# Moving the f operand loads and the result stores of a down projection from SyncE's DMA queue to GpSimd's

## Chip, cores and metric

The kernel runs on one core of one Trainium2 chip. The metric is the device time of one execution in microseconds (us), and the smaller one is better. Engines are called as in the profile: PE is TensorE (PEld its weight loads), DVE is VectorE, ACT is ScalarE, POOL is GpSimd, SP is SyncE. SP computes nothing here: its program is a list of DMA issues in a fixed order. POOL can issue DMAs as well.

## The reference

One decoder layer, float32, for 512 tokens of width 2048: two attention mixers with a residual, then a feed-forward part with a gated causal convolution. The change lies in the last product of the second part.

```
D_MODEL = 2048; SEQ = 512; D_FF = 5632

def conv_ffn(h, w_up, w_conv, b_conv, w_down):
    S = h.shape[1]
    u = h @ w_up
    up = jnp.pad(u, ((0, 0), (CONV_W - 1, 0), (0, 0)))
    conv = b_conv
    for j in range(CONV_W):
        conv = conv + w_conv[j] * up[:, j:j + S]
    gate, val = jnp.split(conv, 2, axis=-1)
    return (jax.nn.silu(gate) * val) @ w_down
...
    x = x + gt_a * y                                   # after the mixers
    h = rms_norm(x, g_ffn[l]) * (1.0 + sc_f) + sh_f
    x = x + gt_f * conv_ffn(h, w_up[l], w_conv[l], b_conv[l], w_down[l])
```

Below, f is `silu(gate) * val`, 5632 x 512, stored with features on the partitions.

## The kernel before

**Number format.** Every float32 operand is split into a rounded part hi and a rest lo (`split`: ACT writes hi on L130, DVE writes lo = operand - hi on L131), and each product is three matmuls (L1082 to L1084: hi x hi, hi x lo, lo x hi). So each weight and each activation passes ACT and DVE before TensorE can use it. The splits of weights appear as `whi` and `wlo` in the profile, those of f operands as `slot<-slot`.

**The product scheme.** `seven` computes a 2 x 2 block product with seven block products instead of eight, in the manner of Strassen. One `Pair` covers two blocks of 128 output rows by 512 tokens. It loads four raw weight blocks (`load`, L968, on SP's queue), forms sums of them on DVE (`comb`, L981), splits the seven results, and runs seven steps on TensorE. After each step the result leaves the PSUM bank: ACT copies (L985 here, L987 in the up projection) or DVE adds (L991, L993). `seven` prepares the weights of a step `AHEAD` steps before that step, here 3. The right-hand operands are seven combinations of f (`KINDS`: r11, t3, t2, r21, t1, t4, r22), each 128 x 256 per block of the contraction.

**Up projection.** As each pair of f tiles is complete, `f_out` (stores on L1397 and L1406) writes f and its combinations to DRAM tiles `f_d` from POOL's queue.

**Down projection.** The contraction of 5632 is cut into four chunks (`DH` = 5, 6, 6 and 5 double blocks). For each chunk the eight column pairs are run in turn, `down_pair(c, j)`: 8 x 7 = 56 steps a chunk, in the order of `KINDS` within a pair. At the end of a pair, `fin` adds its two tiles into DRAM (`x1_d`) by an accumulating DMA from POOL (L1553). In the last chunk, x1 is loaded back (L1544, POOL), added (L1550, DVE), and the result is stored to `out` (L1551).

**The f operands.** A chunk's split operands stay in SBUF during its 56 steps, in tiles from a common pool of slots (`get` and `put`; a tile put back may be taken again after some steps). `ahead` is called after every step. It calls `load_tile` (L1482: up to two DMAs of 128 x 256 from `f_d` into one slot) and `split_tile` (L130 and L131 into two further slots) for the tiles of this and the next chunk. A load is asked for up to nine tiles ahead; a split is made no earlier than four steps after its load, unless the operand is due in two steps or less. In the last steps of a chunk the operands of that chunk become free one kind after the other (`held_by`), and the loads and splits for the next chunk pile up around that place.

**Order.** The program is written as above, but every engine's own order is decided by a planner (`TileContext(nc, schedule_with_timeline_sim=True)`) from its estimates of durations. Each engine and each DMA queue then runs its list strictly in order, and a DMA whose slot is not yet free holds up everything behind it in its queue. Weights (`raw<-in_w_down`), f loads and result stores share SP's list; stores of f, accumulates and x1 loads share POOL's.

The switch from up to down is `turn()`: it lays out seven raw buffers and four pairs of hi and lo buffers, of 768 columns each, for the weights.

Of the kernel before, what the change touches and what calls it, by code (L numbers as in the profile page):

```python
# [18 lines left out]
P = 128  # L19
T = 512  # L20
D = 2048
KD = D // P
# [9 lines left out]
def trunk_layer_kernel(  # L32
# [21 lines left out]
    V, A, G, PE, SP = nc.vector, nc.scalar, nc.gpsimd, nc.tensor, nc.sync  # L54
# [14 lines left out]
    def get(dt=F32):  # L69

        i = min(free, key=lambda n: rested[n])
        free.remove(i)
        if cur[i] is None or cur[i].dtype != dt:
            cur[i] = pool.tile([P, T], dt, name=f"slot{i}", tag=f"slot{i}")
        held[id(cur[i])] = i
        return cur[i]

    def getr():
        return get(F32R)

    def put(*ts, lag=2):

        for t in ts:
            i = held.pop(id(t))
            rested[i] = clock[0] + lag
            free.append(i)
# [126 lines left out]
    def late_loads():  # L213
        SP.dma_start(posi, rows(positions))
        for j in range(3):
# [17 lines left out]
                    base=0, pattern=[[-1, P]], channel_multiplier=1)  # L233
# [35 lines left out]
    for ks in (range(0, 7), range(7, 14), range(14, KD)):  # L269
# [4 lines left out]
        for k in ks:  # L274
            t = get()
# [112 lines left out]
    for g in range(-2, 8):  # L388
# [7 lines left out]
        if 0 <= g + 1 < 8:  # L396
            ada_cols(g + 1)
            for k in (2 * g + 2, 2 * g + 3):
                hi, lo, t = getr(), getr(), ht[k % 2]
# [138 lines left out]
    for tb in range(1, 4):  # L538
        S = (tb + 1) * P
        qiT = []  # L540
        for cb in range(2):
            t = qi[tb, cb]
# [4 lines left out]
            o = (getr(), getr())  # L547
# [60 lines left out]
    for tb in range(4):  # L608
        t = kva[tb]
# [299 lines left out]
    HT = T // 2  # L909
# [188 lines left out]
    for i in range(KH // 2):  # L1098
        raw = [get() for _ in range(4)]
        ta, tb_ = get(), get()  # L1100
        for j in range(2):
            k, o = 2 * i + j, slice(j * HT, (j + 1) * HT)
# [262 lines left out]
    for k in range(KD):  # L1365
        t = x1T[k]
# [23 lines left out]
    f_d = [[dram.tile([P, T if n else HT], F32, name=f"f{n}_{i}") for n in range(4)] for i in range(NF_ // 2)]  # L1390
# [79 lines left out]
    base = [sum(DH[:c]) for c in range(len(DH))]  # L1470
# [5 lines left out]
    def load_tile():  # L1476
        c, n, i = tiles.popleft()
        t = get()
        m, o = KEPT[n]
        w = min(2, DH[c] - i)  # L1480
        for e in range(w):
            SP.dma_start(t[:, e * HT:(e + 1) * HT], f_d[base[c] + i + e][m][:, o * HT:(o + 1) * HT])  # L1482
        coming.append((c, n, t, w * HT, clock[0]))

    def split_tile():
# [10 lines left out]
    def ahead(step, last):  # L1496

        first = [sum(56 for _ in DH[:c]) for c in range(len(DH))]

        def due(c, n):  # L1500
            return first[c] + KINDS.index(n) - step

        for late in (False, True):
            if coming and coming[0][0] <= last:
                c, n, _, _, at = coming[0]
                if due(c, n) <= 2 or not late and clock[0] >= at + 4 and rests(4) and len(free) >= 2 + KEEP \
                        and (due(c, n) < 12 or step % 2 == 0):
                    split_tile()
        for _ in range(2):
            if tiles and tiles[0][0] <= last:  # L1510
                c, n, _ = tiles[0]
                if due(c, n) <= 5 or len(coming) < (9 if due(c, n) < 24 else 4) and rests(3) and len(free) > KEEP:
                    load_tile()
# [22 lines left out]
    def down_pair(c, j):  # L1536
        ns = (2 * j, 2 * j + 1)
        x1 = []

        def load(blk):  # L1540
            if c == len(DH) - 1 and not x1:
                for n in ns:
                    x1.append(get())
                    G.dma_start(x1[-1], x1_d[n])  # L1544
            return w_downs[c][j, blk]

        def fin(*us):
            for i, (n, u) in enumerate(zip(ns, us)):
                if x1:
                    V.tensor_tensor(u, u, x1[i], ALU.add)  # L1550
                    SP.dma_start(out[n * P:(n + 1) * P, :], u)  # L1551
                else:
                    G.dma_start(x1_d[n], u, accum_op=ALU.add)  # L1553
            put(*us, lag=6)
            put(*x1)

        o = ops[c]
        return Pair(tuple(o[n] for n in ("r11", "r21", "r22", "t1", "t2", "t3", "t4")), load, fin, K=DH[c],
                    scale=tuple(mod[:, 80 + n:81 + n] for n in ns))
# [75 lines left out]
```

## Time and profile before

| | |
|---|---|
| median of 3 runs | 2737.32 us (2736.68 to 2745.78) |
| the profiled execution's own time | 2737.34 us |
| its span in the profile | 2735.6 us |
| mean granted TensorE clock | 0.985 |
| busy: PE, DVE, ACT, POOL | 2629.2, 2182.8, 1281.8, 272.0 us |
| f loads (`slot<-f`, L1482, SP) | 154 of 128 KB |
| weights of the down projection (L968, SP) | 64 of 384 KB and 64 of 320 KB |
| accumulates (L1553, POOL) | 48 of 256 KB |
| result stores (L1551, SP) | 16 of 256 KB |
| last f load of the profile issued at | 2608.4 us |

TensorE is busy for 96% of the span, but that is an average: the question for this change is what it does in the stretches in which it pauses. The down projection begins at about 2222 us, when the last step of the up projection has freed the weight buffers. A timeline row gives start, duration, engine, line, operation, tiles and shapes; in brackets stands how long the engine had been idle before the instruction, and what ended that wait. For the queues SPq and POOLq the duration is that of issuing, with consecutive issues of one kind put together.

### The profile page before, as it was taken

Reading aid. Unit: us, or ns where it says so; the run is one execution under the profiler, and the core shown is the slowest. Engines: PE = TensorE matmul, PEld = TensorE weight load, DVE = VectorE, ACT = ScalarE, POOL = GpSimd, SP = SyncE. Lnnn points to the kernel's source line nnn. Section 1 sums busy time; section 2 is a strip of 40 time slices with the busy share of each in tenths; the row PEclk is TensorE's granted clock in tenths of the full one; section 3 lists DMA queues with packets and bytes.
Section 4 is the critical chain, followed back from the end, with each engine's and each line's share of the span. In section 5 each row is a group of like instructions: output and inputs, shape, how many; then the busy total and the mean of one; then the engine's idle time right before and its main releaser. Section 6 shows DMA issues by size and latency. Waiting matters only on the chain.

```text
span 2735.6 us, 45476 instructions
## 1 busy us (share of the span) xinstructions
PE 2629.2 (96%) x17200; PEld 2359.1 (86%) x17200; DVE 2182.8 (80%) x3669; ACT 1281.8 (47%) x2069; POOL 272.0 (10%) x495
## 2 busy tenths in 40 slices
PE   6999999999999999999999999999999988898999
PEld 5787687779997767788789999999999978898999
DVE  7977967698878667973878888889898986777777
ACT  4333434334454465322545555555555564545444
POOL 1001011110032222100100000000000001010110
PEclk8999999999999999999999999999999999999999
DMA  9943136665585578952333333333334365756563
GB/s 339 339 152 105 29 113 214 208 198 177 196 251 163 169 257 289 336 192 96 137 117 132 120 125 129 124 125 135 123 129 142 119 205 142 194 135 182 137 199 114
DMA packets 236240, 464.33 MB, mean 170 GB/s; under 512 B 24330, under 2 KB 85412, under 8 KB 236020
## 3 DMA queue, kind: packets, MB, share of 16 engines
q1 hardware_dynamic: 199348, 368.79, 41.6%
q0 software_dynamic: 36640, 92.63, 12.1%
q8 instruction: 134, 2.20, 0.3%
q14 instruction: 86, 0.70, 0.1%
q10 hardware_dynamic: 32, 0.01, 0.0%
HBM read 397.11 MB, written 64.23 MB: 169 GB/s over the span
## 4 chain that ended last, share of the span: by engine, by line
PE 55%; issue 21%; DVE 11%; DMA 9%; POOL 2%; ACT 1%; SPq 0%; POOLq 0%; DVEq 0%; ACTq 0%
PE bank L134 10%; PE bank L135 10%; PE bank L136 10%; PE bank L1082 7%; PE bank L1083 7%; PE bank L1084 7%; DMA raw<-in_w_ups 4%; DVE wlo L131 4%; DMA slot<-in_w_ada 2%; POOL x L1553 1%; DVE raw L981 1%; DVE slot L981 1%; DVE slot L1380 1%; DMA raw<-in_w_down 1%; PE bank L1233 1%
## 5 line engine op out<-in xcount | busy, mean ns | idle before, releaser
L1082 PE MATMUL bank<-slot,whi 128*128 128x256 f32 x3920 | 1114.6, 285 | 61.7 <-ACT whi L130 17.9
L1083 PE MATMUL bank<-slot,whi 128*128 128x256 f32 x3920 | 1107.2, 283 | 0.2 <-DVE slot L131 0.2
L1084 PE MATMUL bank<-slot,wlo 128*128 128x256 f32 x3920 | 1097.4, 283 | 2.9 <-DVE wlo L131 2.8
L1082 PEld LDWEIGHTS bank<-slot,whi 128*128 128x128 f32 x3920 | 748.7, 191 | 77.7 <-ACT whi L130 19.9
L1083 PEld LDWEIGHTS bank<-slot,whi 128*128 128x128 f32 x3920 | 748.4, 191 | 0.7 <-DVE slot L131 0.5
L1084 PEld LDWEIGHTS bank<-slot,wlo 128*128 128x128 f32 x3920 | 742.6, 191 | 4.2 <-DVE wlo L131 4.1
L130 ACT ACTIVATE whi<-raw 128x1024 fp32r<-128x1024 f32 (+2 forms) x458 | 424.4, 928 | 463.9 <-PE bank L1083 367.9
L131 DVE TENSOR_TENSOR wlo<-raw,whi 128x1024 fp32r<-128x1024 f32 (+2 forms) x458 | 481.3, 1056 | 60.8 <-ACT whi L130 59.2
L122 ACT ACTIVATE whi<-raw 128x1024 fp32r<-128x1024 f32 (+4 forms) x182 | 187.4, 1031 | 389.2 <-PE bank L136 202.3
L123 DVE TENSOR_TENSOR wlo<-raw,whi 128x1024 fp32r<-128x1024 f32 (+4 forms) x182 | 215.6, 1186 | 145.4 <-ACT whi L122 140.1
L981 DVE TENSOR_TENSOR raw<-raw,raw 128x1024 f32<-128x1024 f32 (+2 forms) x252 | 264.7, 1051 | 71.1 <-DMA raw<-in_w_down 44.2
L135 PE MATMUL bank<-wlo,slot 128*128 128x512 f32 (+2 forms) x768 | 297.4, 388 | 0.9 <-DVE wlo L123 0.9
L134 PE MATMUL bank<-whi,slot 128*128 128x512 f32 (+2 forms) x768 | 289.9, 390 | 6.6 <-ACT slot L401 4.0
L136 PE MATMUL bank<-whi,slot 128*128 128x512 f32 (+2 forms) x768 | 292.3, 384 | 0.0
L135 PE MATMUL bank<-slot,whi 128*128 128x512 f32 (+1 forms) x656 | 262.9, 401 | 1.4 <-DVE slot L703 1.3
L134 PE MATMUL bank<-slot,whi 128*128 128x512 f32 (+1 forms) x656 | 260.9, 403 | 3.3 <-ACT slot L1370 2.3
L136 PE MATMUL bank<-slot,wlo 128*128 128x512 f32 (+1 forms) x656 | 257.5, 401 | 0.0
L134 PEld LDWEIGHTS bank<-whi,slot 128*128 128x128 f32 x768 | 146.0, 190 | 37.8 <-ACT slot L401 4.1
L135 PEld LDWEIGHTS bank<-wlo,slot 128*128 128x128 f32 x768 | 146.3, 191 | 29.5 <-DVE wlo L123 1.4
L136 PEld LDWEIGHTS bank<-whi,slot 128*128 128x128 f32 x768 | 145.1, 189 | 28.5 <-issue 0.3
L739 DVE SCALAR_TENSOR_TENSOR slot<-slot,c_act,slot 128x512 f32<-128x512 f32 x203 | 148.9, 746 | 24.9 <-DMA slot<-in_w_ada 23.9
L130 ACT ACTIVATE whi<-slot 128x512 fp32r<-128x512 f32 x204 | 128.1, 629 | 82.9 <-PE bank L1083 63.3
(292 smaller groups left out, 3007.1 us busy)
## 6 DMA issues: line engine op xcount, KB each, us to landing
slot<-in_w_ada SPq DMA_DIRECT2D x344, 256.0 KB, 5.7
raw<-in_w_ups SPq DMA_DIRECT2D x126, 512.0 KB, 4.4
raw<-in_w_in SPq DMA_DIRECT2D x50, 512.0 KB, 3.6
raw<-in_w_down SPq DMA_DIRECT2D x64, 384.0 KB, 4.0
raw<-in_w_down SPq DMA_DIRECT2D x64, 320.0 KB, 3.7
slot<-f SPq DMA_DIRECT2D x154, 128.0 KB, 3.4
slot<-in_w_ups SPq DMA_DIRECT2D x68, 256.0 KB, 2.6
f<-slot POOLq DMA_DIRECT2D x66, 256.0 KB, 5.3
```

Of the source, the lines that this page charges most:

```text
L122: A.activation(hi, raw[:, :w], AF.Copy)
L123: V.tensor_tensor(lo, raw[:, :w], r32(hi), ALU.subtract)
L130: A.activation(dst_hi, src, AF.Copy)
L131: V.tensor_tensor(dst_lo, src, r32(dst_hi), ALU.subtract)
L134: PE.matmul(o, lh, rh, start=first, stop=False)
L135: PE.matmul(o, lh, rl, start=False, stop=False)
L136: PE.matmul(o, ll, rh, start=False, stop=last)
L739: V.scalar_tensor_tensor(acc, ts[i], c_act[:, k:k + 1], acc, op0=ALU.mult, op1=ALU.add)
L981: V.tensor_tensor(part(o, x, y), part(a, x, y), part(b, x, y), op)
L1082: PE.matmul(o, wh[:, ks], rh, start=first and k == 0, stop=False, skip_group_check=True)
L1083: PE.matmul(o, wh[:, ks], rl, start=False, stop=False, skip_group_check=True)
L1084: PE.matmul(o, wl[:, ks], rh, start=False, stop=last, skip_group_check=True)
```

## The change

The loads of f operands (L1482) are issued by POOL (`G`) in place of SP. The result stores of the last chunk (L1551) are issued by POOL too, but for those of the last column pair, which stay on SP. Nothing else of the program text changes. SP's list falls by 168 instructions (154 f loads and 14 stores), and POOL's grows by 168. As the planner sees other queues, it also orders ACT, DVE and PE somewhat differently from the end of the up projection on; the instructions themselves are the same in number and shape.

```
@@ -1479,7 +1479,7 @@
         m, o = KEPT[n]
         w = min(2, DH[c] - i)
         for e in range(w):
-            SP.dma_start(t[:, e * HT:(e + 1) * HT], f_d[base[c] + i + e][m][:, o * HT:(o + 1) * HT])
+            G.dma_start(t[:, e * HT:(e + 1) * HT], f_d[base[c] + i + e][m][:, o * HT:(o + 1) * HT])
         coming.append((c, n, t, w * HT, clock[0]))
 
     def split_tile():
@@ -1548,7 +1548,7 @@
             for i, (n, u) in enumerate(zip(ns, us)):
                 if x1:
                     V.tensor_tensor(u, u, x1[i], ALU.add)
-                    SP.dma_start(out[n * P:(n + 1) * P, :], u)
+                    (SP if j == KD // 2 - 1 else G).dma_start(out[n * P:(n + 1) * P, :], u)
                 else:
                     G.dma_start(x1_d[n], u, accum_op=ALU.add)
             put(*us, lag=6)
```

More of the change, by code (lines that the diff above doesn't have):

```diff
@@ L1481, in load_tile @@
         for e in range(w):
-            SP.dma_start(t[:, e * HT:(e + 1) * HT], f_d[base[c] + i + e][m][:, o * HT:(o + 1) * HT])
+            G.dma_start(t[:, e * HT:(e + 1) * HT], f_d[base[c] + i + e][m][:, o * HT:(o + 1) * HT])
         coming.append((c, n, t, w * HT, clock[0]))
@@ L1550, in fin @@
                     V.tensor_tensor(u, u, x1[i], ALU.add)
-                    SP.dma_start(out[n * P:(n + 1) * P, :], u)
+                    (SP if j == KD // 2 - 1 else G).dma_start(out[n * P:(n + 1) * P, :], u)
                 else:
```

## The prediction

> **What bounds the kernel now.** I read the busy time by stretch first, for the stage that holds the moved transfers: the end of the up projection and the down projection, from 2200 us to the end. The columns are the stretch, its length, then busy time of PE, PEld, DVE, ACT and POOL, the granted TensorE clock, the DMA share and GB/s.
>
> ```profile
> 2200.00:2240.00 40.00, 30.50 (x227) 28.76 (x226) 38.32 (x60) 29.46 (x53) 1.63 (x3) 0.91 0.73 228
> 2240.00:2300.00 60.00, 50.23 (x385) 49.15 (x386) 41.57 (x62) 24.52 (x41) 6.58 (x8) 0.94 0.57 136
> 2350.00:2400.00 50.00, 43.45 (x319) 42.57 (x320) 39.40 (x54) 25.02 (x41) 5.15 (x6) 0.90 0.69 176
> 2400.00:2470.00 70.00, 68.23 (x567) 67.45 (x566) 51.59 (x66) 34.23 (x53) 6.82 (x8) 1.00 0.62 153
> 2470.00:2510.00 40.00, 32.39 (x234) 31.77 (x233) 28.59 (x43) 21.52 (x38) 3.41 (x4) 0.87 0.72 202
> 2600.00:2650.00 50.00, 45.01 (x359) 44.19 (x360) 35.40 (x52) 23.75 (x40) 12.29 (x20) 0.97 0.72 213
> 2650.00:2735.60 85.60, 81.19 (x681) 80.80 (x680) 67.76 (x101) 39.59 (x67) 0.00 (x0) 0.99 0.37 123
> ```
>
> Inside a chunk TensorE is the bound: 68.23 us busy of 70, at clock 1.00. What can be won lies where it isn't. I put the loss of a stretch at its idle time plus (1 - clock) times its busy time. That is 9.5 + 2.7 = 12.2 us for 2200 to 2240 (up turns into down), 9.8 + 3.0 = 12.8 for 2240 to 2300 (start of chunk 0), 6.6 + 4.3 = 10.9 for 2350 to 2400 (chunk 0 to 1), 7.6 + 4.2 = 11.8 for 2470 to 2510 (chunk 1 to 2), and 5.0 + 1.4 = 6.4 for 2600 to 2650 (chunk 2 to 3). In the last stretch 4.4 us are idle, almost all behind the last matmul.
>
> Next, the timeline of PE: its pauses in those stretches, each with what ended it in brackets.
>
> ```profile
> 2249.62 0.39 PE L1082 MATMUL bank<-slot,whi 128*128 128x256 f32 x1 [2.18 <-ACT whi L130]
> 2261.92 0.39 PE L1082 MATMUL bank<-slot,whi 128*128 128x256 f32 x1 [2.72 <-DVE slot L991]
> ...
> 2352.16 0.58 PE L1082 MATMUL bank<-slot,whi 128*128 128x256 f32 x1 [3.35 <-DVE slot L991]
> 2364.89 0.41 PE L1082 MATMUL bank<-slot,whi 128*128 128x256 f32 x1 [1.90 <-ACT slot L985]
> 2372.59 0.39 PE L1082 MATMUL bank<-slot,whi 128*128 128x256 f32 x1 [1.89 <-ACT whi L130]
> 2488.34 0.58 PE L1082 MATMUL bank<-slot,whi 128*128 128x256 f32 x1 [3.32 <-ACT whi L130]
> 2502.27 0.58 PE L1082 MATMUL bank<-slot,whi 128*128 128x256 f32 x1 [3.53 <-ACT slot L985]
> 2638.32 0.58 PE L1082 MATMUL bank<-slot,whi 128*128 128x256 f32 x1 [2.58 <-DVE slot L991]
> ```
>
> DVE and ACT end the pauses, so I ask what these two had waited for. First the table of waits from 2200 us on (us in total, times, longest), then the rows of the longest ones.
>
> ```profile
> POOL x L1553 <- DVE slot L991: 271.9, 24, 17.2
> DVE raw L981 <- DMA raw<-in_w_down: 44.2, 28, 4.4
> ACT slot L130 <- DMA slot<-f: 30.2, 15, 5.8
> ```
> ```profile
> 2350.02 0.96 DVE L981 TENSOR_TENSOR raw<-raw,raw 128x768 f32<-128x768 f32 x1 [3.53 <-DMA raw<-in_w_down]
> 2371.17 0.63 ACT L130 ACTIVATE slot<-slot 128x512 fp32r<-128x512 f32 x1 [5.82 <-DMA slot<-f]
> 2486.93 0.63 ACT L130 ACTIVATE slot<-slot 128x512 fp32r<-128x512 f32 x1 [4.49 <-DMA slot<-f]
> ```
>
> Before 2352 a weight came late for L981; before 2364 to 2373 and before 2488 ACT stood at the split of an f tile for a chunk that PE had not reached, with splits of weights that PE needed at once behind it in ACT's order. The timeline of the DMA queue on SP, and one row of POOL, says why those transfers were late.
>
> ```profile
> 2255.39 0.80 SPq L1482 DMA_DIRECT2D slot<-f  x2
> 2256.30 15.73 SPq L968 DMA_DIRECT2D raw<-in_w_down  x4
> ...
> 2337.22 7.04 SPq L1482 DMA_DIRECT2D slot<-f  x8
> 2344.36 0.86 SPq L968 DMA_DIRECT2D raw<-in_w_down  x2
> ...
> 2368.50 1.74 SPq L1482 DMA_DIRECT2D slot<-f  x4
> 2370.34 15.51 SPq L968 DMA_DIRECT2D raw<-in_w_down  x6
> ```
> ```profile
> 2362.99 0.86 POOL L1553 DMA_DIRECT2D x<-slot  x1 [3.20 <-ACT slot L985]
> ```
>
> The waits of the same queue name the cause of the gap before 2368.50:
>
> ```profile
> SPq L1482 <- DMA x<-slot: 30.8, 10, 5.8
> ```
>
> Two forms of one thing: f loads in front of weights. Eight f loads took 7.04 us to issue, and the weights whose lateness DVE shows at 2350.02 came out only then. From 2362.99 to 2368.50 the next f load waited (5.8 us at most, ten times in all) for the accumulate issued at 2362.99 to finish reading the slot that it writes, and six weights queued behind it. The same pattern stands at 2255.39, with four weights behind.
>
> **The change, part by part.** The 154 f loads (L1482) leave SP for POOL. The issue rows, in ns (min/median/max), and the time from issue to landing in us:
>
> ```profile
> L1482 SPq DMA_DIRECT2D slot<-f x154: 319/382/1457, 2045.7 to 2608.4; - x154
> L1406 POOL DMA_DIRECT2D f<-slot x66: 542/542/556, 1409.4 to 2241.7; - x66
> ```
> ```profile
> slot<-f SPq DMA_DIRECT2D x154, 128.0 KB, 3.4
> ...
> slot<-x POOLq DMA_DIRECT2D x16, 256.0 KB, 6.6
> ```
>
> SP loses 154 x 0.382 = 59 us of issuing, POOL gains 154 x 0.542 = 83 us, with room: POOL issued for 6.8 us in the 70 us from 2400. Landing on POOL is bounded by 3.4 us (as on SP) and 6.6 us (the x1 load, twice the bytes, in a crowded stretch); I take about 5. A tile is asked for at least four steps before its split unless it is urgent, and a step lasts about 123 / 56 = 2.2 us (the 56 steps of a chunk lie between the pauses at 2364.89 and 2488.34), so 1.6 us more landing is covered by some 9 us. If that cover is gone, ACT waits, as in the second rival.
>
> What SP's freedom is worth, from below: nothing, if weights were late for another cause. From above: all of the loss of both chunk changes (10.9 + 11.8) and, in chunk 0, the two pauses 2.18 and 2.72 with half of that stretch's clock loss (1.5): 22.7 + 6.4 = 29.1 us. Between these I take the row that is nearest to a chunk change after the edit. That is chunk 2 to 3: SP holds almost only weights there, while POOL loads x1 in bursts of 256 KB, and the loss is 6.4 us and not 0. The reason is in these two stretches (same columns as above), one with f loads, one with x1 loads from POOL:
>
> ```profile
> 2480.00:2487.00 7.00, 5.02 (x43) 4.81 (x41) 5.16 (x8) 2.23 (x6) 0.00 (x0) 1.00 1.05 356
> 2620.00:2626.00 6.00, 4.74 (x40) 4.54 (x39) 3.81 (x6) 1.48 (x2) 2.99 (x6) 1.00 1.03 393
> ```
>
> In both the 16 DMA engines are full (shares 1.05 and 1.03), whoever issued. So I let each chunk change fall to 6.4: a gain of 4.5 + 5.4 = 9.9 us. In chunk 0 the f load at 2255.39 and the weights behind it part: the pause of 2.72 and 1.5 of clock go, 4.2 us; the pause of 2.18 is ACT waiting for an f load and stays.
>
> POOL is in order too. Its new order has f loads behind stores of f and behind accumulates, which wait up to 17.2 us for DVE. But the loads behind them are for the next chunk, tens of steps away, or reuse the accumulate's own slot and would have waited on SP as well. I cost this at 0, between -2 and the second rival's price.
>
> The planner also moves work on ACT and DVE, since it orders all engines by its own estimate. In the built order DVE has 13 splits of f tiles within the first 14 steps of the down projection, where it had 8:
>
> ```profile
> L131 DVE TENSOR_TENSOR slot<-slot,slot 128x512 fp32r<-128x512 f32 (+1 forms) x81 | 50.1, 641 | 24.3 <-ACT slot L130 16.1 <-DMA x<-slot 6.2 <-PE bank L1084 1.9
> ```
>
> Five more at 0.641 are 3.2 us. DVE is busy for 38.32 of 40 us there, so they count in full: +3.2. At the chunk changes the built order spreads the same splits more thinly between weights, worth 0 to 3; I leave that in the range.
>
> Fourteen of the 16 result stores (L1551) go to POOL, behind the last x1 loads, and no weight is late beside them now: from 2650 on PE is busy for 81.19 us, and what is missing lies behind the last matmul. The last pair's stores, which set the end, stay on SP. Worth 0, and at most the 14 x 0.16 us of dearer issue, on an engine that nobody waits for then. In the up projection the first f loads now share POOL with stores of f; the loads begin 180 us ahead of their use, so 0.
>
> **Sum.** 9.9 + 4.2 - 3.2 = 10.9 us gained on the profiled execution's 2737.34: 2726.4. That execution equals the median of the runs (2737.32), so nothing is added.
>
> **The rivals.** *The queue was all of it.* Weights on a queue of their own land in time whatever POOL loads, and spread splits of f never hold ACT. For it: the 7.04 us at 2337.22 and the queue blocked to 2368.50 are SP's alone. Against: the x1 row of 2638.32, a pause of 2.58 us with weights nearly alone on SP. Gain 29.1 - 3.2 = 25.9, time 2711.4.
>
> *POOL holds the f loads back, ACT holds the weights.* ACT's order still sets f splits in front of urgent weight splits. If an f load lands more than about 9 us after its place in the program (a blocking accumulate plus 5 us landing is enough), each of the pauses that ACT ends is met twice: 2.18 + 1.90 + 1.89 + 3.32 + 3.53 = 12.8 us more, and 8.5 more of clock loss as at both chunk changes now. Against that only the weight pauses go, 2.72 + 3.35 = 6.1, and DVE's 3.2 is added: 12.8 + 8.5 - 6.1 + 3.2 = 18.4 us slower, 2755.7. For it: ACT waited 5.82 us for one f load already. Against: most such loads were late behind SP's own block, and POOL idles.
>
> *The data path, not the queue, was late.* If the 1.05 share is what delays weights at both changes, the same bytes arrive together in any order; all pauses stay, and DVE's 3.2 is added: 2740.5. The rows for it are the two full stretches; against it is 0.88 us per f load at 2337.22, over twice the 0.382 of the instruction. The Trainium skill, "DMA: Bandwidth & Descriptors", section "Issuing engines are not separate DMA queues", says that DMAs from the scalar, sync and gpsimd engines end up on the same 16 DMA engines, and that several issuers save only the sequencer's initiating time. By that rule this rival is the case; the trace agrees with it at the two full stretches, not at 2362.99 to 2368.50, where a queue stood still for a semaphore.
>
> That the change doesn't do what it says is excluded: in the built order SP has only weights and the last pair's stores.
>
> **How the numbers follow.** Forecast 0.36, queue was all 0.27, POOL holds back 0.25, data path 0.12. What a measurement here can tell from no change is 0.5%, 13.7 us. Faster by more: the first rival and 0.08 of the forecast, whose own range is 2713 to 2737: 0.35. Slower by more: 0.25. Within: 0.28 + 0.12 = 0.40. The range for 8 in 10 goes from a little below the first rival (29.1 gained with nothing given back is 2708) to 2754, just short of the second rival's 2755.7: 2706 to 2754.
>
> **What would show it.** Right: SP rows of L1482 gone; no weight issued behind a wait for an accumulate; the pauses at the first two chunk changes down to 5 us each, clock 0.95 or more; the wait of L981 for weights under 30 us. Wrong upward: ACT's wait for f loads above 30.2 us, f loads landing after 6.6 us, POOL standing at L1553 with urgent loads behind. Wrong downward: chunk changes with no pause above 1 us.

## The result, and the profile after

The changed kernel takes 2712.66 us (median of 4 runs, 2708.11 to 2715.54), against 2737.0 us before (median of 4 too). The ratio is 0.9902, with a 95% interval of 0.9878 to 0.9927: 1.0% faster, 24 us. The profiled execution took 2708.11 us, the fastest of the four, so its trace shows 29 us and not 24 of difference; the interval covers both.

First the stretches, as in the prediction (busy PE, PEld, DVE, ACT, POOL; granted clock; DMA share; GB/s). The chunk changes come earlier now, so the last three windows are moved by 15, 20 and 25 us.

```profile
2200.00:2240.00 40.00, 31.14 (x235) 29.56 (x234) 36.33 (x56) 25.99 (x46) 25.99 (x49) 0.91 0.70 220
2240.00:2300.00 60.00, 56.84 (x467) 55.61 (x466) 51.29 (x79) 34.13 (x59) 14.98 (x23) 1.00 0.68 176
2335.00:2385.00 50.00, 44.99 (x356) 43.83 (x356) 40.41 (x56) 27.26 (x45) 19.90 (x33) 0.97 0.72 203
2450.00:2490.00 40.00, 37.96 (x314) 37.35 (x314) 34.51 (x50) 24.19 (x41) 18.15 (x31) 1.00 0.76 212
2575.00:2625.00 50.00, 46.56 (x386) 45.80 (x385) 38.32 (x56) 24.58 (x42) 15.00 (x25) 1.00 0.75 228
```

By the same measure, idle time plus (1 - clock) times busy time, the losses are 11.7, 3.2, 6.4, 2.0 and 3.4 us; they were 12.2, 12.8, 10.9, 11.8 and 6.4. That is 27.4 us less in these five. The two largest gains are 9.8 us at the second chunk change, where 5.4 were forecast, and 9.6 us at the start of chunk 0, where 4.2 were forecast. The pauses of PE that are over 2 us from 2230 us on are two, where there were seven:

```profile
2340.62 0.58 PE L1082 MATMUL bank<-slot,whi 128*128 128x256 f32 x1 [3.12 <-DVE slot L991]
2597.77 0.39 PE L1082 MATMUL bank<-slot,whi 128*128 128x256 f32 x1 [3.12 <-DVE slot L991]
```

The table of waits from 2180 us on (total, times, longest), PE's rows of before first:

```profile
PE bank L1082 <- ACT whi L130: 15.7, 6, 5.8
PE bank L1082 <- DVE slot L991: 14.7, 10, 3.4
PE bank L1082 <- ACT slot L985: 12.2, 13, 3.5
```

For after, with the first part of the page:

```profile
DVE raw L981 <- DMA raw<-in_w_down: 47.5, 26, 3.9
PE bank L1082 <- DVE slot L991: 13.1, 9, 3.1
PE bank L1082 <- ACT whi L130: 6.7, 2, 5.6
PE bank L1082 <- ACT slot L985: 4.9, 9, 1.1
ACT slot L130 <- DMA slot<-f: 1.2, 3, 0.5
```
```profile
PE 2613.8 (97%) x17200; PEld 2345.9 (87%) x17200; DVE 2180.2 (81%) x3669; ACT 1281.9 (47%) x2069; POOL 363.6 (13%) x663
```

Two lines stand against each other here. ACT's wait for f loads went from 30.2 us to 1.2. But the wait of L981 for weights, which a queue of their own should have cured, is 47.5 us, where it was 44.2. And of the 29.3 us by which the span is shorter, 13.9 are idle time of PE, and 15.4 are its busy time, which fell from 2629.2 us for the same 17200 matmuls: the mean granted clock rose from 0.985 to 0.990, as fewer of them run at half clock behind a long pause. (2.3 us of the busy time went before 2180 us, where idle time grew by as much; from there on, PE is 16.1 us less idle and 13.2 us less busy.)

So the weights did not become more punctual, and yet the time fell. The timelines of DVE and of SP's queue show what makes a weight late now, ahead of the pause at 2340.62:

```profile
2333.75 0.82 DVE L131 TENSOR_TENSOR wlo<-raw,whi 128x640 fp32r<-128x640 f32 x1
2337.87 0.96 DVE L981 TENSOR_TENSOR raw<-raw,raw 128x768 f32<-128x768 f32 x1 [3.31 <-DMA raw<-in_w_down]
```
```profile
2334.59 0.33 SPq L968 DMA_DIRECT2D raw<-in_w_down  x1
```

DVE is done with a raw buffer at 2333.75 + 0.82 = 2334.57; SP, with no f load in its list, issues the next weight at 2334.59; it lands, and L981 starts 3.28 us later, with L991 behind it. The weight waited for one of the seven raw buffers, not for a place in a queue. The waits of SP's queue from 2200 us on say the same in sum, first of before, then of after: SP now stands at the buffers where it issued f loads.

```profile
SPq L968 <- DVE raw L981: 147.1, 23, 11.4
SPq L968 <- DVE wlo L131: 114.6, 71, 12.2
```
```profile
SPq L968 <- DVE wlo L131: 251.8, 90, 16.9
SPq L968 <- DVE raw L981: 150.2, 29, 12.3
```

Times to landing grew a little: f loads 3.8 us (median) from POOL against 3.4 from SP, weights of 384 KB 5.1 against 4.0. How much of the weights' lateness is a late buffer and how much a slower transfer isn't separated by these rows.

```profile
raw<-in_w_down SPq DMA_DIRECT2D x64, 384.0 KB, 5.1
raw<-in_w_down SPq DMA_DIRECT2D x64, 320.0 KB, 4.2
slot<-f POOLq DMA_DIRECT2D x154, 128.0 KB, 3.8
```

### The profile page after: what moved, and what is told of

It is laid out like the page before. It is cut to its first block, busy times and chain, and to the rows that moved or that the text cites. A ratio compares the mean times of both kernels' runs of the same rounds, so it can differ in the third digit from the quotient of the medians.

```text
span 2706.3 us, 45437 instructions
## 1 busy us (share of the span) xinstructions
PE 2613.8 (97%) x17200; PEld 2345.9 (87%) x17200; DVE 2180.2 (81%) x3669; ACT 1281.9 (47%) x2069; POOL 363.6 (13%) x663
## 4 chain that ended last, share of the span: by engine, by line
PE 53%; DVE 16%; issue 15%; DMA 13%; POOL 2%; ACT 1%; SPq 0%; DVEq 0%; POOLq 0%; ACTq 0%
PE bank L134 9%; PE bank L135 9%; PE bank L136 9%; PE bank L1082 7%; PE bank L1083 7%; PE bank L1084 7%; DVE wlo L131 6%; DMA raw<-in_w_ups 5%; DMA slot<-in_w_ada 2%; DMA raw<-in_w_down 2%; DVE raw L981 2%; DVE slot L981 1%; DVE slot L1380 1%; DMA raw<-in_w_in 1%; DVE slot L1381 1%
## 5 line engine op out<-in xcount | busy, mean ns | idle before, releaser
L981 DVE TENSOR_TENSOR raw<-raw,raw 128x1024 f32<-128x1024 f32 (+2 forms) x252 | 265.2, 1053 | 68.7 <-DMA raw<-in_w_down 47.5
```

The source lines that it names most:

```text
L981: V.tensor_tensor(part(o, x, y), part(a, x, y), part(b, x, y), op)
```

## The experiments

**What else the change moves.** The planner orders ACT, DVE and PE anew when a transfer changes its queue. In the built orders, the splits of f on ACT stand between other splits of weights as follows. Each number is one f split (81 from the last steps of the up projection on), and says how many splits of down weights precede it; only the starts of chunks 0, 1 and 2 are listed.

```
          chunk 0 (behind 22 and 15 zeros)
before    3 3 4 4 6 6 6 7 8 15 22
after     1 4 4 6 6 6 7 8 8 12 13 14 16 16 16 19 23 24
          chunk change 0 to 1
before    53 54 54 54 55 56 57 57 58 58 58 58 59 61 61 62 62 69
after     53 54 54 54 55 58 58 58 59 61 62 63 65 65 65 69 72 73
          chunk change 1 to 2
before    108 109 110 110 110 112 112 113 113 114 114 114 115 115 116 117 119 125
after     108 110 110 110 111 114 114 114 115 115 117 117 118 120 121 122 127 128
```

At the change from chunk 0 to 1, 16 splits of f have 54 to 62 weight splits in front of them before, and 10 after. Besides these places, the order of the rest (weight splits, sums, matmuls) differs too. So there are two theories. *Queue theory*, mine: f loads on SP held weights and themselves back. *Order theory*, the rival: the queue is beside the point, and the gain is the planner's new order. They can be told apart by edges that fix an engine's order without adding a wait:

```
+def pin(tc, nc):
+    info = mybir.DependencyInfo(mybir.DependencyClass.NoSync, mybir.DependencyReason.DATA)
...
+        for a, b in zip(names, names[1:]):
+            tc.add_manual_dep(traced[b], a, info, reason="pin")
...
     down_run()
+    pin(tc, nc)
```

`names` lists the instructions of PE, DVE and ACT from the end of the up projection on. The first four runs, e1 to e4, were made side by side; every ratio is to the kernel before in runs of the same round. No run holds a kernel to its own order, so that the edges cost nothing by themselves is assumed and not shown.

**e1: queue of before, order of after.** The kernel before, with `names` from the changed kernel. SP's own list isn't held: how f loads and weights stand in it is again the planner's choice.

> f loads and result stores stay on SP as in the kernel before, but TensorE, VectorE and ScalarE are held to exactly the order that they have in the changed kernel (edges of order alone, no waits). Queue theory (the f loads are late because they stand in SP's list among weights that wait for buffers): the gain of 24 us is gone, 2730 to 2740, and ACT waits for f loads about 30 us as before. Order theory (the planner merely put the splits of f further behind their loads): the gain stays, 2708 to 2718, and ACT's wait for f loads is under 5 us. A value in the middle divides the gain between the two.

Measured: 2719.16 us, ratio 0.9936 (0.9919 to 0.9953). Waits:

```profile
DVE raw L981 <- DMA raw<-in_w_down: 58.7, 28, 6.5
PE bank L1082 <- DVE slot L991: 21.8, 17, 4.1
PE bank L1082 <- ACT whi L130: 6.7, 2, 5.6
PE bank L1082 <- ACT slot L985: 4.5, 8, 1.3
ACT slot L130 <- DMA slot<-f: 1.7, 2, 1.4
```

Without any transfer moved, 0.64% of the 0.98% is there, 17.5 us, and ACT's wait for f loads is gone with f loads still on SP. The time lies a microsecond above the band of the order theory and far from that of the queue theory, which falls for the larger part.

**e2: queue of after, order of before.** The changed kernel, with `names` from the kernel before.

> f loads and 14 result stores on POOL as in the changed kernel, but TensorE, VectorE and ScalarE are held to the order of the kernel before. Queue theory: 2708 to 2718, ACT's wait for f loads under 5 us. Order theory: 2730 to 2740, ACT's wait for f loads near 30 us. If the gain needs both: above 2725 here and in the run with the other order on SP.

Measured: 2743.57 us, ratio 1.003 (1.0016 to 1.0044): slower by 8 us, and above even the band of the order theory. With the order of before, the queue change loses. ACT's wait stays, and at chunk change 0 to 1 the old chain of events is back with POOL in SP's part (timeline rows of POOL, ACT and PE):

```profile
ACT slot L130 <- DMA slot<-f: 31.8, 15, 5.6
PE bank L1082 <- ACT whi L130: 21.1, 9, 6.1
```
```profile
2364.03 2.16 POOL L1482 DMA_DIRECT2D slot<-f  x4 [0.62 <-PE bank L1084]
2366.69 0.88 POOL L1553 DMA_DIRECT2D x<-slot  x1 [0.50 <-ACT slot L985]
...
2372.04 0.54 POOL L1482 DMA_DIRECT2D slot<-f  x1 [2.29 <-DMA x<-slot]
```
```profile
2376.60 0.63 ACT L130 ACTIVATE slot<-slot 128x512 fp32r<-128x512 f32 x1 [5.57 <-DMA slot<-f]
```
```profile
2378.01 0.58 PE L1082 MATMUL bank<-slot,whi 128*128 128x256 f32 x1 [3.61 <-ACT whi L130]
```

The f load still waits until the accumulate has left the slot that it reuses, whichever queue it is in; the split at 2376.60 still stands in front of a weight split; PE pauses for 3.61 us, where it paused for 1.89 at 2372.59 before.

**e3 and e4: the two halves of the change.** e3 has the first hunk of the diff alone, e4 the second alone; nothing is pinned, so each has the planner's own order.

> Only the f loads go to POOL, all 16 result stores stay on SP. If the stores are worth nothing, as predicted: 2708 to 2718. If they carry part of the gain: above 2720.

> Only 14 result stores go to POOL, all f loads stay on SP. As predicted 0: 2734 to 2740. If the stores carry part of the gain, under 2730.

Measured: e3 2714.16 us, ratio 0.9924 (0.9909 to 0.9938); e4 2733.05 us, ratio 0.9994 (0.9981 to 1.0008). e4's time is a microsecond below its band, but its interval holds no change: the stores are worth nothing that can be measured, as predicted, and the f loads' hunk brings the gain, with the order that comes with it. The intervals of e3 and e1 (0.9936) overlap, so what POOL adds to the new order is small.

**e5 and e6: which part of the order.** Both have f loads and stores on SP. e5 takes the order of before, and moves only the 63 f splits of chunks 1 to 3, on ACT and DVE, to the places of after (counted in other instructions of the engine). e6 takes the order of after, and puts all f splits back to the places of before. Only the lists in `names` differ from e1's.

> f loads and stores on SP; TensorE, VectorE and ScalarE in the order of the kernel before, except that the 63 splits of f for chunks 1 to 3 stand at the places, counted in other instructions, at which the changed kernel has them (mostly later, behind up to 11 more splits of weights). Place theory (ACT stood at f splits whose loads had not landed, with urgent weights behind): 2718 to 2726, ACT's wait for f loads under 10 us. Step theory (the other difference of the orders, that the planner breaks fewer steps of TensorE apart, brings the gain): 2733 to 2740.

> f loads and stores on SP; TensorE, VectorE and ScalarE in the order of the changed kernel, except that all splits of f stand at the places of the kernel before. Place theory: 2730 to 2740, ACT's wait for f loads 25 us or more. Step theory: near 2719, as with the whole order of the changed kernel on SP.

Measured: e5 2729.85 us, ratio 0.9978 (0.9963 to 0.9992); e6 2726.39 us, ratio 0.9962 (0.9949 to 0.9974). Each theory had claimed the whole, and neither gets it: the places bring 0.22%, the rest of the order 0.38%, together 0.60%, and e1 had 0.64%. On SP the two add up within their intervals. They aren't exact complements: the 18 splits of f at the start of chunk 0 stand at the places of after in e1 alone. Their waits differ. Of e5:

```profile
DVE raw L981 <- DMA raw<-in_w_down: 53.3, 31, 3.4
PE bank L1082 <- ACT whi L130: 7.9, 4, 5.4
ACT slot L130 <- DMA slot<-f: 1.9, 3, 1.2
```

and of e6:

```profile
DVE raw L981 <- DMA raw<-in_w_down: 30.7, 22, 3.5
ACT slot L130 <- DMA slot<-f: 21.0, 13, 4.8
PE bank L1082 <- DVE slot L991: 5.7, 5, 2.4
```

The places take away ACT's wait for f loads (30.2 to 1.9) and halve the pauses of PE that ACT's weight splits end (15.7 to 7.9). The rest of the order leaves 21.0 us of ACT's wait (25 or more was expected), and in this trace it works on DVE's side: L981 waits 30.7 us instead of 44.2, and the pauses that L991 ends fall from 14.7 to 5.7. L981 and L991 share DVE's list, and an L981 that stands early waits for its weight with L991 behind it, as the row at 2350.02 before shows. But e6's trace is of its fastest execution, 2718.62 us, and e1, which has both parts, waits longer on DVE's side than before (58.7 and 21.8 us, in its slowest execution). So by which wait the rest of the order gains stays open.

**e9 and e10: the same two on POOL.** The lists of e5 and e6, with the change's two hunks.

> f loads and 14 stores on POOL; TensorE, VectorE and ScalarE in the order of the kernel before, with the 63 splits of f for chunks 1 to 3 at the places of the changed kernel (the order of the run e5, which took 2730 with f loads on SP). If f loads from POOL cost time only where ACT stands at them early, the 7 us that POOL cost in the old order are gone: 2724 to 2731. If POOL is dearer whatever the places: 2735 to 2740.

> f loads and 14 stores on POOL; the order of the changed kernel, with all splits of f at the places of the kernel before (the order of e6, 2726 with f loads on SP). If POOL's later loads cost where ACT stands at them early: 2730 to 2738, and ACT's wait for f loads above 25 us. If the old order of steps was what made POOL dear: 2718 to 2724.

Measured: e9 2735.03 us, ratio 0.9984 (0.9969 to 0.9999); e10 2742.39 us, ratio 1.0024 (1.0012 to 1.0036). By time, e9 lies at the lower edge of the dearer band, though its ratio can't be told from e5's (0.9978); e10 lies above both of its bands. In e10 ACT's wait is 30.9 us, as expected, with its longest at 7.1:

```profile
ACT slot L130 <- DMA slot<-f: 30.9, 16, 7.1
PE bank L1082 <- ACT whi L130: 18.7, 5, 5.5
```

All ratios to the kernel before, by queue of the f loads and by order:

| order of PE, DVE, ACT | f loads on SP | f loads on POOL |
|---|---|---|
| before | 1 | 1.0030 |
| before, f splits of chunks 1 to 3 at after's places | 0.9978 | 0.9984 |
| after, f splits at before's places | 0.9962 | 1.0024 |
| after | 0.9936 | 0.9902 (the change) |

Where f splits stand early, POOL costs 0.3 to 0.6%; where they stand late in chunks 1 to 3 only, nothing that can be told; with the whole new order the difference is 0.34% in POOL's favour, from runs not made side by side and with half-widths of 0.17% and 0.25%. So a gain of the queue itself is seen only under the order that the planner made for that queue, and it is about 9 us with an error almost as large. On POOL the parts of the order don't add up: from 1.0030, the places bring 0.46% and the rest 0.06%, but both bring 1.28%. No run here shows why.

**e7 and e8: a rule of distance in the program text.** The kernel before (e7) and the changed one (e8), with splits no earlier than eight steps behind their loads.

```
-                if due(c, n) <= 2 or not late and clock[0] >= at + 4 and rests(4) and len(free) >= 2 + KEEP \
+                if due(c, n) <= 4 or not late and clock[0] >= at + 8 and rests(4) and len(free) >= 2 + KEEP \
...
-                if due(c, n) <= 5 or len(coming) < (9 if due(c, n) < 24 else 4) and rests(3) and len(free) > KEEP:
+                if due(c, n) <= 8 or len(coming) < (9 if due(c, n) < 24 else 4) and rests(3) and len(free) > KEEP:
```

> The kernel before with another planning rule in its text, f loads on SP: a tile is split no earlier than eight steps after its load instead of four, and asked for three steps earlier where it is due (two limits go from 2 and 5 to 4 and 8). If the distance in the text is what counts, 2715 to 2728 and ACT's wait for f loads halved; if the planner's own order undoes it (it moves splits ahead wherever its estimate has the load landed), 2732 to 2740.

> The changed kernel with the same rule of eight steps. ACT already waits for f loads for 1 us only, so by the place theory there is little left: 2706 to 2714, same as the changed kernel. If the remaining pauses come from f splits crowding the weights at the chunk changes, 2700 to 2706.

Measured: e7 2725.68 us, ratio 0.9961 (0.9948 to 0.9974), ACT's wait 22.4 us; e8 2724.03 us, ratio 0.9953 (0.9939 to 0.9967). Without moving a transfer, the rule on SP gains 11 us. That is in the expected band, but ACT's wait fell from 30.2 us by a quarter and not by half, so the gain isn't shown to come from it. On POOL the rule loses against the change, 0.51% by the ratios, outside both expectations: ACT waits 14.0 us for f loads again, in the order that the planner makes of the new rule.

```profile
ACT slot L130 <- DMA slot<-f: 14.0, 6, 6.2
PE bank L1082 <- ACT slot L985: 15.0, 9, 4.3
```

**e11: smaller bursts.** The changed kernel with `len(coming) < 6` in place of 9, and the two limits of e7 (4 and 8 steps), without the distance of eight.

> The changed kernel with at most six f tiles under way near a chunk change instead of nine, each asked for three steps earlier where it is due and split two steps earlier. If bursts of f loads beside the weights make the pauses that are left at the chunk changes: 2700 to 2708 and the wait of L981 for weights under 40 us. If the planner's new order decides, anything from 2712 to 2728.

Measured: 2719.2 us, ratio 0.9935 (0.992 to 0.995); L981's wait is 44.5 us. The bursts are not shown to make the pauses that are left; it is yet another order of the planner, and no better than the change.

**e12: twice the f traffic.** The changed kernel with its order kept, and behind each f load:

```
+            G.dma_start(spare[0], f_d[base[c] + i + e][m][:, o * HT:(o + 1) * HT])
+            spare.rotate(-1)
```

> The changed kernel with its order of TensorE, VectorE and ScalarE kept, and after every f load a second transfer of the same 128 KB from POOL into DRAM that nobody reads: 154 more transfers, 20 MB more read and written. If the shared DMA engines make the weights late (data path): the wait of L981 for weights rises from 47 to 65 us or more, and the time is 2722 to 2740. If only queues matter, weights have their own: L981 stays at 45 to 52 us, and the time within 2710 to 2720.

Measured: 2722.91 us (2712.2 to 2725.56), ratio 0.9943 (0.9927 to 0.996), 11 us above the change. The profiled execution is the fastest of them, 2712.2 us, and L981 waits 51.5 us in it, so the trace doesn't show where the median's 11 us went. The time speaks for the data path, L981's wait against it, and the added issues take places in POOL's list as well: it stays open how much of the weights' lateness is shared bandwidth. It bounds the matter: 20 MB more, read and written, cost 0.4%, with an error of 0.3. That more raw buffers would help was not tried.

No variant beat the change; e3, which lacks the moved stores, can't be told from it.

## Why the prediction was right or wrong

The sign was right, the measured 2712.66 lies in the range, and the forecast of 2726.4 took less than half of the gain. The reason given for the gain was mostly wrong, so the range held by its width and by luck. Two of the signs set for being right came true (idle time of 5.0 and 2.0 us at the first two chunk changes, clock 0.97 and 1.00), the third, L981's wait under 30 us, did not.

**"What SP's freedom is worth" (9.9 + 4.2 us): failed.** With the order of before held it is worth -8 us (e2); under the new order it is about +9, with an error almost as large. I read rows in which f loads stood in front of weights on SP as the cause. Of the two things that were late in them, the weights stay late on a queue of their own (47.5 us against 44.2; under 30 was the sign I had set), as at 2334.59, where DVE had just freed the buffer, and the f loads stay late at the slot that an accumulate still reads, as in e2 (in the change itself POOL waits 16.3 us for it, in four places). I had written that such loads "would have waited on SP as well", but didn't draw the conclusion for POOL: the block moves along, and POOL's list takes 0.54 us an issue.

**"Spreads the same splits more thinly between weights, worth 0 to 3": failed, and this is the main step.** The whole new order is worth 17.5 us on SP (e1): about 6 for the places of the f splits (e5) and 10 for the rest (e6), which the prediction has no term for. For the places it had the sizes in hand. It had traced PE's pauses of 1.90, 1.89 and 3.32 us to ACT standing at an f split with weights behind it, and it knew that the built order moves these splits back. It priced the load's lateness and not the place of the wait in ACT's list.

**"Five more at 0.641 are 3.2 us" for DVE at the start: failed.** DVE was busy for 36.33 us of 40 there, less than the 38.32 of before, and the loss went from 12.2 to 11.7. The price was put on the wrong stretch: in its rows from 2200 to 2240 us DVE has 25 splits of f before and 20 after, and the later ones fall into the start of chunk 0, where DVE was busy for 41.57 us of 60 before and 51.29 after, while PE gained.

**Chunk changes and chunk 0: too small, and by the wrong reason.** A loss of 6.4 us each was forecast, 6.4 and 2.0 were measured, and 3.4 instead of 6.4 at the third, for which no gain was forecast. Chunk 0: 4.2 forecast, 9.6 measured; the pause of 2.18 that "stays" went too. The prediction also left out a third pause of chunk 0, of 2.56 us; after the change the longest in that stretch is 1.49 us:

```profile
2293.55 0.58 PE L1082 MATMUL bank<-slot,whi 128*128 128x256 f32 x1 [2.56 <-DVE slot L991]
```
```profile
2290.34 0.69 DVE L131 TENSOR_TENSOR slot<-slot,slot 128x512 fp32r<-128x512 f32 x1 [3.43 <-DMA x<-slot]
```

Here DVE stands at a split of f whose slot an accumulate still reads, with L991 behind it: again the place of a split, and no weight on SP.

**Stores 0: right** (e4, 0.9994). **f loads landing at about 5 us:** 3.8 measured, so the cover was never short because of landing.

**The rivals.** *The queue was all of it* was named at 2711.4, and its time is the nearest one, by luck; its mechanism is not the one at work (L981 still waits 47.5 us). *POOL holds the f loads back* does not describe the change, but it does describe e2 and e10: ACT's wait of 31.8 and 30.9 us, 0.30 and 0.24% slower, 7 to 8 us, where 18.4 were priced. Which of the two occurred was decided by the order. *The data path*: by the rule of the Trainium skill ("DMA: Bandwidth & Descriptors", "Issuing engines are not separate DMA queues") the change of issuer alone should gain next to nothing. e2 agrees in that nothing is gained, but the 8 us that it loses are not in the rule; the change as a whole gains by something that this rule does not speak of. The rival's own time, 2740.5, is near e2's 2743.57, but for another reason: the pauses of PE that ACT's weight splits end grew, from 15.7 us to 21.1.

**The clock.** From 2180 us on, 13.2 of the 29.3 us of the traced gain are busy time, as matmuls run at full instead of half clock (granted clock 0.97 before and 0.99 after, from 2230 us on). The Trainium skill ("TensorE: Matmul & The Clock Gate", "What's actually happening") puts the fall to half clock at an idle window of about 3.4 us that runs freely. The trace agrees in that length alone does not decide: of two pauses of 3.12 us after the change, one is followed by a matmul of 0.58 us and the other by one of 0.39. It does not agree on the length: before the change, pauses of 2.56 us (2293.55) and 2.58 us (2638.32) were enough, and the granted clock is 0.50 from 2293.50 to 2296. Here each microsecond of pause taken away brought about 0.8 us of busy time (16.1 and 13.2).

## What to carry to other kernels

Where a planner orders the engines, moving a DMA to another queue is two changes: compare the built orders, and hold one of them fixed (edges of order without waits) before crediting the queue. On an engine that runs its list in order, a wait for data that is needed much later holds up urgent work behind it (28 us of such waits went in e5, and 6 us of time with them); the remedy is its place in the list, and it can be had without moving a transfer. A wait for a slot that is still being read goes along with the transfer to the queue that issues it, as in e2.

## What the runs showed of the hardware that was not expected

A 128 KB load took about as long from POOL's queue as from SP's: 3.8 us in median against 3.4, for the same 154 loads. And 154 more transfers of 128 KB beside the down projection (e12) cost 11 us in median, with executions between 2712.2 and 2725.56 us, although the DMA engines were full at the chunk changes before (share 1.05 at 2480).
